# A second product added into its copy in place ahead of the last turns, and GpSimd in program order in the output projection

## The chip, the cores and the metric

The kernel runs on one core of a Trainium2 chip. The metric is the device time of one execution in microseconds (us). Three executions of the kernel before were timed, and one more was profiled.

## The reference

A decoder of two layers on 1,024 positions of width 1,024, in float32. Each layer mixes (sparse attention in the first layer, forgetting attention in the second, and a small cross-attention in both), projects the heads back onto the residual stream, normalizes it, and adds a gated feed-forward part with a causal convolution of width 3. What the change touches is the output projection and the start of the feed-forward part:

```python
x = x + jnp.concatenate([o_mix, o_mem], axis=-1) @ w_o[l]
x = x + conv_ffn(rms_norm(x, ffn_norm[l]), w_up[l], conv_w[l], conv_b[l], w_down[l])
# in conv_ffn
u = h @ w_up
u = lax.conv_general_dilated(u, conv_w[:, None, :], window_strides=(1,), padding=[(CONV_WIDTH - 1, 0)], ...) + conv_b
a, b = u[..., :D_FF], u[..., D_FF:]
return (jax.nn.silu(a) * b) @ w_down
```

## The kernel before

**Matmuls.** Every float32 operand is split into a rounded high part and the rest (`split`, lines 76 to 84: ScalarE writes the high part at L81, VectorE the low part at L82), and a product is three matmuls, L157, L158 and L159. So each operand costs one ScalarE and one VectorE instruction before TensorE can use it.

**Output projection** (`out_proj`). The residual stream `x` lies in SBUF as eight row tiles t = 0 to 7, in two column halves n. For each n and t, 24 matmuls fill a PSUM tile `psb`, which VectorE adds onto `x` (L871). In the second half (n = 1) a row tile is then complete, and `norm_part` follows: a DMA stores it (`xm`, L909), ScalarE sums its squares (L118), VectorE scales the sum (L119, `ss`), GpSimd raises it to the power -1/2 (L121, `rs`), and VectorE multiplies the tile by it in place (L911), which waits for the store too. From t = 4 on VectorE forms differences with the tile four below (L931, L932, L929) and GpSimd one more (L930). TensorE transposes the results (`turn_split`, L903, called a turn here) into `psb`, from where they are split into the operands of the next stage (`hx` and `hT`). The pool of `psb` has four buffers.

**Up-projection** (class `Up`). The product of the hidden state and `w_up` is made of seven half-size products per channel tile instead of eight (Strassen's scheme in Winograd's form), for NF = 22 pairs n of channel tiles. Pair n loads two weight blocks, `ra` and `rb` (L1272, 512 KB each, into the ring `wr` of three buffers). GpSimd forms sums of their halves: `sums_21` (L1279, L1280) and `sums_34` (L1286, L1287), each into one tile `ws` of a ring of two. ScalarE and VectorE split these and the weights themselves (`split_a`, `split_21`, `split_34`, `split_b`). The products of a pair go to the two halves `p` and `c` of a PSUM tile `psa`, of which there are two:

- `first` fills `p` and copies it to an SBUF tile c1 (L1320; tag `c`, a ring of three buffers).
- `second` fills another tile q, which `take_second` adds to c1 into `u` (L1338).
- `third` adds onto `p`, and copies it (L1320, c2). Product 3 fills `c` and is copied too (c5). Products 4, 5 and 6 follow.

For the pairs 0 and 1 `first` and `second` run inside `out_proj`, and there q is the half `c` of their `psa`. `u` lies in the pool of the feed-forward part, which takes the memory of `x` once the last turn has read it, so `take_second` of both pairs stands at the start of `run`, behind all turns.

**What waits for what.** The framework places a wait where two instructions touch the same tile, and takes a PSUM tile `psa` as one thing: product 3 of pair 0, which writes the half `c`, waits for `take_second(0)`, and for the copy c2 of the half `p`.

**What sets the order.** In `out_proj` the framework's scheduler orders the instructions of each engine. In `run` a table of slots (`todo`) does, and `manual_schedule` keeps VectorE and ScalarE in program order there.

Of the kernel before, what the change touches and what calls it, by code (L numbers as in the profile page):

```python
# [8 lines left out]
F32 = mybir.dt.float32  # L9
# [3 lines left out]
ALU = mybir.AluOpType  # L13
# [4 lines left out]
P = 128  # L18
D = 1024
S = 1024  # L20
NT = S // P
KT = D // P
CH = 512
# [19 lines left out]
class Trunk:  # L43
# [398 lines left out]
    def attention(self, ap, l, od, units, work, spare, lead=4, lag=2, lead_work=2):  # L442
# [79 lines left out]
        for k in range(first, len(steps) + lag + 4):  # L522
            st = steps[k] if 0 <= k < len(steps) else None
            run(k, "max")
            if st:
                self.turn_p(ap, st)
            run(k, "exp")
            if st:
                self.lower_p(st)
            run(k, "norm")  # L530
            while items and items[0]["at"] <= k:
                begin(k, items.pop(0))
            if k < 0 and lead_work and items:
                for _ in range(lead_work):
                    if work:
                        advance()
            if st and k < n_fill:
                owed += max(total, 0) / (n_fill - k)
                while owed >= 1 and work:
                    owed -= 1  # L540
                    advance()
            if 0 <= k - lag < len(steps):
                self.value(steps[k - lag])
                if steps[k - lag]["end"]:
                    finish(k, steps[k - lag]["u"])
            if not work and whole and k % 4 == 0:
                operand()
            if k == units[-1]["start"]:
                w_o = self.load_block(self.a["w_o"][l], [(0, CH)])
# [298 lines left out]
    def out_proj(self, l, oT, pool, fx, up):  # L848

        nc, a = self.nc, self.a
        (oT, w), B, late, gb = oT, up.B, [], None
        for n in range(2):
            if n:
                w = self.load_block(a["w_o"][l], [(CH, CH)])
                gb = self.wraw([P, D])
                nc.sync.dma_start(gb, a["ffn_norm"][l:l + 1, :].to_broadcast([P, D]))
                up.load(0)
            for t in range(NT):  # L860
                ps = self.psb()
                oh, ol = oT[t // 4]
                o = (t % 4) * P
                for kt in (0, 1, 2, 3, 4, 6, 7, 5):
                    self.mm3(ps, (oh[:, kt, o:o + P], ol[:, kt, o:o + P]), w(kt, 0, CH), kt == 0, kt == 5)
                if n == 0 and t == NT - 1:
                    up.conv_turn()
                if n and t == NT - 1:
                    up.split_a(0)
                xs = self.x[:, t, n * CH:(n + 1) * CH]  # L870
                nc.vector.tensor_tensor(xs, ps, xs, ALU.add)  # L871
                turns, late = late, self.norm_part(pool, fx, l, t, gb, B) if n else []
                if n and t in (2, 4):
                    (up.sums_21 if t == 2 else up.sums_34)(0)
                if n and t == 1:
                    turns, late = [], turns + late
                for f in turns:
                    f()
        up.load(1)
        up.first(0)  # L880
        up.second(0, True)
        late[0]()
        up.split_a(1)
        up.split_21(0)
        up.first(1)
        for f in late[1:]:
            f()
        up.second(1, True)
        for i in range(4):
            self.turn_split(self.x[:, 4 + i, CH:], B["t3"], i)  # L890
            self.turn_split(self.x[:, i, CH:], B["t4"], i)
            if i == 1:
                up.third(0)
                up.split_34(0)
                up.split_b(0)
                up.sums_21(1)
                up.sums_34(1)
# [226 lines left out]
    def gated(self, l, oT, src, fx):  # L1124

        tc = self.tc
        with tc.tile_pool(name=f"e{l}", bufs=1) as ep:
            up = Up(self, l, ep)
            with tc.tile_pool(name=f"x{l}", bufs=1) as xp:
                self.residual(xp, src)  # L1130
                self.out_proj(l, oT, xp, fx, up)
            down = Down(self, l, up.gds, fx)
            with tc.tile_pool(name=f"u{l}", bufs=1) as late, tc.manual_schedule(engines={mybir.EngineType.DVE, mybir.EngineType.Activation}):
                up.run(late, down)
        return down
# [64 lines left out]
    def run(self):  # L1200
        a, tc = self.a, self.tc
        self.constants()
        self.xd = self.dp.tile([S, D], F32, name="xd")
        self.xm = [self.dp.tile([S, D], F32, name=f"xm{l}") for l in range(2)]
        oT = self.layer1_attn(*self.middle(self.layer0()))
        with tc.tile_pool(name="fx1", bufs=1) as fx:
            down = self.gated(1, oT, self.xd, fx)
            with tc.tile_pool(name="y1", bufs=1) as yp:
                gb = []

                def each(j):
                    if j == 0:
                        gb.append(self.gain(yp, a["final_norm"].rearrange("(o n) -> o n", o=1)))
                    if j % 3 == 2:
                        self.final(yp, gb[0], j // 3)
                halves = {}

                def late(j):
                    if j == 0:
                        self.final(yp, gb[0], 3)  # L1220
                    if 2 <= j < 6:
                        halves[j + 2] = self.final_right(yp, gb[0], j + 2)
                self.down_all(1, down, yp, each, lambda: None, True, late)
                for t in range(4, NT):
                    self.final_left(yp, gb[0], t, *halves[t])


class Up:
# [106 lines left out]
    def take_second(self, n):  # L1335
        s, k = self.st[n], self.k
        s["ua"] = k.sb(self.late, [P, S], F32, "u", 3)
        k.nc.vector.tensor_tensor(s["ua"][:, :CH], s["q"], s["c1"], ALU.add)  # L1338

    def third(self, n):  # L1340
        s = self.st[n]
        self.prod(n, s["p"], "s2", "t2", False)
        s["c2"] = self.copied(s["p"])
# [64 lines left out]
    def run(self, late, down):  # L1408


        self.late = late
        done = {0: 3, 1: 3}
        self.split_21(1)
        self.take_second(0)
        self.take_second(1)
        self.third(1)
        todo = {}

        def at(slot, f, *args):
            todo.setdefault(slot, []).append(lambda: f(*args))  # L1420
        for slot, f in ((148, down.claim_x), (150, down.claim_x), (152, down.claim_h), (154, down.claim_h), (156, down.claim_h),
                        (158, down.claim_x), (160, down.claim_h)):
            at(slot, f)
        at(151, down.fetch, 3)
        for slot, n in ((151, 1), (153, 2), (155, 3), (159, 4)):
            at(slot, down.prep, n)
        for n in range(NF):
            for slot, f in ((-9, self.load), (-6, self.sums_21), (-3, self.sums_34), (-3, self.split_a), (-2, self.split_21),
                            (-1, self.split_b), (3, self.split_34)):
                if n > 1 or n == 1 and f in (self.split_b, self.split_34):  # L1430
                    at(7 * n + slot, f, n)
            for slot, h, tap in ((11, 0, 1), (12, 0, 0), (13, 1, 1), (14, 1, 0)):
                at(7 * n + slot, self.conv, n, h, tap)
            at(7 * n + 16, self.gate, n)
            if n % 2:
                at(7 * n + 17, self.left, n // 2)
                at(7 * n + 19, self.store, n // 2)
        for slot in range(7 * NF + 13):
            for f in todo.pop(slot, ()):
                f()  # L1440
            for n in (slot // 7 - 1, slot // 7):
                i, odd = divmod(slot - 7 * n, 2)
                if 0 <= n < NF and not odd and done.get(n, 0) <= i < 7:
                    self.product(n, i)
            if slot >= 7 * NF + 6:
                down.step()
        assert not todo
# [163 lines left out]
```

## Time and profile before

| what | value |
|---|---|
| median of the timed runs | 2577.46 us |
| the three runs | 2571.35, 2577.46, 2578.0 us |
| the profiled execution | 2576.98 us |
| its span in the trace | 2574.9 us |
| granted TensorE clock, mean | 0.99 |
| busy: TensorE, VectorE, ScalarE, GpSimd | 2467.4, 1880.5, 1347.7, 745.7 us |

The span starts with the first instruction in the trace and ends with the last; 2.1 us of the execution's time lie outside it. Busy time of TensorE counts matmuls that overlap each other. PE is TensorE, DVE VectorE, ACT ScalarE, POOL GpSimd, SP the engine that issues the DMAs. In a row of the timeline stand the start, the duration, the engine, the line, the instruction with what it writes and reads, and in brackets how long the engine sat idle before it and what ended that. Names are given without buffer numbers.

### The profile page before, as it was taken

The numbers are of one execution on the slowest core, as the hardware profiler recorded it, in microseconds if no ns is written. First come the engines' busy times: TensorE is split into PE (matmuls) and PEld (weight loads), VectorE is DVE, ScalarE is ACT, GpSimd is POOL, SyncE is SP. The second block draws the span as 40 slices with busy tenths as digits, with TensorE's granted clock in tenths as the row PEclk, the third lists the DMA queues.
The fourth block names the chain that finished last, engine by engine and source line by source line (L and its number), as shares of the span: only waits on it lengthen the run. The fifth ranks groups of instructions, "written<-read, shape, count | busy, mean of one in ns | idle before, by whom it ended". The sixth has DMA issues, their size and how long they took to land.

```text
span 2574.9 us, 35712 instructions
## 1 busy us (share of the span) xinstructions
PE 2467.4 (96%) x12306; PEld 2059.2 (80%) x12306; DVE 1880.5 (73%) x3180; ACT 1347.7 (52%) x2565; POOL 745.7 (29%) x616
## 2 busy tenths in 40 slices
PE   7898999988999999999999999999899999999998
PEld 6787877777778888887888988887677888888887
DVE  5757888887367878877766467878466787888866
ACT  5337777877145445444454356767234544545444
POOL 0104444544124554543000000000223555452000
PEclk9998999999999999999999999999999999999999
DMA  8473234433422323347334566766532332338523
GB/s 245 141 218 111 66 87 115 112 103 119 165 74 87 113 95 103 111 136 287 129 126 131 156 181 189 203 182 178 202 115 69 105 112 97 101 113 289 179 90 123
DMA packets 303276, 357.68 MB, mean 139 GB/s; under 512 B 38024, under 2 KB 183288, under 8 KB 303096
## 3 DMA queue, kind: packets, MB, share of 16 engines
q1 hardware_dynamic: 303096, 355.41, 43.8%
q8 instruction: 97, 1.59, 0.3%
q14 instruction: 83, 0.68, 0.1%
HBM read 245.55 MB, written 109.78 MB: 138 GB/s over the span
## 4 chain that ended last, share of the span: by engine, by line
PE 74%; DVE 8%; ACT 6%; DMA 5%; issue 3%; POOL 3%; SPq 1%; POOLq 0%; ACTq 0%; DVEq 0%
PE psa L157 12%; PE psa L158 12%; PE psa L159 12%; PE psb L157 9%; PE psb L159 9%; PE psb L158 9%; PE psa L300 4%; PE psb L399 4%; PE psb L422 4%; ACT pt L406 2%; DVE pt L409 2%; ACT ps L343 1%; DVE wl L82 1%; DVE ps L330 1%; POOL ws L1396 1%
## 5 line engine op out<-in xcount | busy, mean ns | idle before, releaser
L81 ACT ACTIVATE wh<-wr 128x512 fp32r<-128x512 f32 (+2 forms) x254 | 193.4, 765 | 330.1 <-PE psb L159 142.5
L82 DVE TENSOR_TENSOR wl<-wr,wh 128x512 fp32r<-128x512 f32 (+2 forms) x254 | 243.5, 963 | 141.3 <-ACT wh L81 140.5
L1377 DVE SCALAR_TENSOR_TENSOR v<-u,cw,v 128x1023 f32<-128x1023 f32 (+1 forms) x176 | 277.3, 1575 | 68.9 <-ACT v L1375 67.3
L409 DVE TENSOR_TENSOR pt<-psb,pt 128x512 fp32r<-128x512 f32 (+2 forms) x380 | 247.3, 660 | 70.1 <-ACT pt L406 66.9
L1375 ACT ACTIVATE v<-u,cw 128x1024 f32<-128x1024 f32 x88 | 109.8, 1248 | 310.2 <-DVE u L1364 283.5
L406 ACT ACTIVATE pt<-psb 128x512 fp32r<-128x512 f32 (+2 forms) x380 | 214.1, 574 | 92.2 <-PE psb L399 86.4
L422 PE MATMUL psb<-pt,vv 128*128 128x512 f32 (+2 forms) x864 | 227.3, 359 | 18.1 <-DVE pt L409 12.3
L157 PE MATMUL psa<-hT,wh 128*128 128x512 f32 x560 | 219.7, 393 | 5.3 <-DVE u L1338 5.3
L159 PE MATMUL psa<-hT,wl 128*128 128x512 f32 x560 | 219.0, 391 | 0.8 <-DVE wl L82 0.8
L158 PE MATMUL psa<-hT,wh 128*128 128x512 f32 x560 | 218.9, 391 | 0.0
L300 PE MATMUL psa<-kk,qq 128*128 128x512 f32 (+4 forms) x792 | 187.0, 351 | 15.5 <-DVE stat L330 7.7
L422 PEld LDWEIGHTS psb<-pt,vv 128*128 128x128 f32 x864 | 142.8, 193 | 43.0 <-DVE pt L409 20.5
L343 ACT ACTIVATE ps<-ps,stat 128x128 f32<-128x128 f32 (+1 forms) x192 | 148.1, 773 | 46.5 <-DVE stat L330 46.3
L481 POOL TENSOR_TENSOR wr<-wr 128x512 f32<-128x512 f32 x32 | 41.7, 1306 | 432.3 <-DMA kd<-st 246.1
L157 PE MATMUL psb<-hT,wh 128*128 128x512 f32 x384 | 156.8, 408 | 1.8 <-DVE pt L409 1.4
L1279 POOL TENSOR_TENSOR ws<-wr 128x512 f32<-128x512 f32 x44 | 72.2, 1640 | 295.6 <-DMA wr<-in_w_up_dram 243.3
L399 PE MATMUL psb<-consts,ps 128*128 128x128 f32 x928 | 149.0, 278 | 8.1 <-DVE pt L409 3.4
L121 POOL TENSOR_TENSOR rs<-ss,consts 128x1 f32<-128x1 f32 x40 | 23.0, 577 | 458.0 <-DVE ss L119 320.2
L159 PE MATMUL psb<-hT,wl 128*128 128x512 f32 x384 | 151.7, 395 | 0.0
L158 PE MATMUL psb<-hT,wh 128*128 128x512 f32 x384 | 151.0, 393 | 0.0
L330 DVE CUSTOM_DVE_ANT_0 ps<-psa,caub 128x128 f32<-128x128 f32 (+1 forms) x192 | 139.0, 751 | 15.0 <-PE psa L300 14.7
L300 PEld LDWEIGHTS psa<-kk,qq 128*128 128x128 f32 x792 | 123.0, 195 | 31.2 <-DVE stat L330 10.0
(299 smaller groups left out, 6822.5 us busy)
## 6 DMA issues: line engine op xcount, KB each, us to landing
wr<-in_w_up_dram SPq DMA_DIRECT2D x88, 512.0 KB
wr<-gd SPq DMA_DIRECT2D x154, 256.0 KB
gd<-v SPq DMA_DIRECT2D x88, 256.0 KB
o<-ob SPq DMA_DIRECT2D x128, 128.0 KB
wr<-o SPq DMA_DIRECT2D x32, 512.0 KB
hT<-in_w_down_dram SPq DMA_DIRECT2D x64, 256.0 KB
gd<-gs SPq DMA_DIRECT2D x60, 256.0 KB
qd<-st SPq DMA_DIRECT2D x56, 256.0 KB
```

What stands on the lines that cost most here:

```text
L81: nc.scalar.activation(hi, src, AF.Copy)
L82: nc.vector.tensor_tensor(lo, src, f32(hi), ALU.subtract)
L157: mm(out, lh, rh, start=first, stop=False, skip_group_check=more)
L158: mm(out, lh, rl, start=False, stop=False, skip_group_check=more)
L159: mm(out, ll, rh, start=False, stop=last, skip_group_check=more)
L300: nc.tensor.matmul(out, w, rhs, start=b not in banks[:i], stop=b not in banks[i + 1:])
L343: nc.scalar.activation(p, p, AF.Exp, bias=st[:, 0, ii:ii + 1], scale=-1.0, accum_out=st[:, 1, ii:ii + 1])
L399: nc.tensor.transpose(tp[0:kb, x:x + P], br["pt"][ii][:, o:o + kb], self.ident)
L406: nc.scalar.activation(st["hi"], st["src"], AF.Copy)
L409: self.nc.vector.tensor_tensor(st["lo"], st["src"], f32(st["hi"]), ALU.subtract)
L422: self.nc.tensor.matmul(out, v, t, start=st["begin"] and i == 0, stop=st["end"] and i == len(mms) - 1)
L1377: nc.vector.scalar_tensor_tensor(v[:, d:], u[:, :S - d], cw[:, tap, i:i + 1], v[:, d:], ALU.mult, ALU.add)
```

## The change

The addition of q to c1 is taken out of `run` and put into `out_proj`, as an addition in place (`take_early`): VectorE reads q and c1 and writes c1. What remains in `run` is a copy of the result into `u`, on GpSimd (`place_early`). And all of `out_proj` keeps GpSimd in program order.

```diff
         for f in late[1:]:
             f()
+        up.take_early(0)
         up.second(1, True)
+        up.take_early(1)
         for i in range(4):
...
-                self.out_proj(l, oT, xp, fx, up)
+                with tc.manual_schedule(engines={mybir.EngineType.Pool}):
+                    self.out_proj(l, oT, xp, fx, up)
...
+    def take_early(self, n):
+        s = self.st[n]
+        self.k.nc.vector.tensor_tensor(s["c1"], s["q"], s["c1"], ALU.add)
+
+    def place_early(self, n):
+        s, k = self.st[n], self.k
+        s["ua"] = k.sb(self.late, [P, S], F32, "u", 3)
+        k.nc.gpsimd.tensor_copy(s["ua"][:, :CH], s["c1"])
...
-        self.take_second(0)
-        self.take_second(1)
+        self.place_early(0)
+        self.place_early(1)
         self.third(1)
```

Both layers run this code. The lines of the changed kernel are some higher: L930 of before is L932, L911 is L913, L1279 to L1287 are L1282 to L1290, L1320 is L1323.

GpSimd, from the second half of the output projection of the first layer on, before. `rs` is the scale of a row tile, `ws` a weight sum of pair 0, `x<-x,t` the difference of L930:

```order
L1279 TENSOR_TENSOR ws_7636<-wr_7529 128x512
L1286 TENSOR_TENSOR ws_7756<-wr_7527,wr_7529 128x512
L121 TENSOR_TENSOR rs_7562<-ss_7559,consts 128x1
L1280 TENSOR_TENSOR ws_7636<-ws_7636,wr_7527 128x512
L1287 TENSOR_TENSOR ws_7756<-wr_7527,ws_7636 128x512
L121 TENSOR_TENSOR rs_7599<-ss_7596,consts 128x1
L121 TENSOR_TENSOR rs_7633<-ss_7630,consts 128x1
L121 TENSOR_TENSOR rs_7698<-ss_7695,consts 128x1
L121 TENSOR_TENSOR rs_7746<-ss_7743,consts 128x1
L930 TENSOR_TENSOR x_7278<-x_7278,t_1317_7753 128x512
L121 TENSOR_TENSOR rs_7804<-ss_7801,consts 128x1
```

The same place after:

```order
L121 TENSOR_TENSOR rs_7564<-ss_7561,consts 128x1
L121 TENSOR_TENSOR rs_7601<-ss_7598,consts 128x1
L121 TENSOR_TENSOR rs_7635<-ss_7632,consts 128x1
L1282 TENSOR_TENSOR ws_7638<-wr_7531 128x512
L1283 TENSOR_TENSOR ws_7638<-ws_7638,wr_7529 128x512
L121 TENSOR_TENSOR rs_7700<-ss_7697,consts 128x1
L121 TENSOR_TENSOR rs_7748<-ss_7745,consts 128x1
L1289 TENSOR_TENSOR ws_7758<-wr_7529,wr_7531 128x512
L1290 TENSOR_TENSOR ws_7758<-wr_7529,ws_7638 128x512
L121 TENSOR_TENSOR rs_7806<-ss_7803,consts 128x1
L932 TENSOR_TENSOR x_7278<-x_7278,t_1317_7755 128x512
```

The scales of the row tiles 0 to 2 stand ahead of pair 0's `sums_21` now, and its `sums_34` behind the scale of row tile 4. With it moves the load of pair 1's `ra`, which takes the buffer that `sums_34` reads: the DMA queue has it behind the stores of row tiles 0 to 4 now, and had it behind that of row tile 0.

GpSimd further on, at the end of the output projection, before. The sums with `wr_79..` are those of pair 1, with `wr_81..` those of pair 2:

```order
L930 TENSOR_TENSOR x_7278<-x_7278,t_1333_7867 128x512
L121 TENSOR_TENSOR rs_7928<-ss_7925,consts 128x1
L1279 TENSOR_TENSOR ws_8096<-wr_7959 128x512
L1280 TENSOR_TENSOR ws_8096<-ws_8096,wr_7957 128x512
L1286 TENSOR_TENSOR ws_8099<-wr_7957,wr_7959 128x512
L1287 TENSOR_TENSOR ws_8099<-wr_7957,ws_8096 128x512
L930 TENSOR_TENSOR x_7278<-x_7278,t_1343_7931 128x512
L1279 TENSOR_TENSOR ws_8180<-wr_8160 128x512
L1280 TENSOR_TENSOR ws_8180<-ws_8180,wr_8158 128x512
```

And after:

```order
L121 TENSOR_TENSOR rs_7930<-ss_7927,consts 128x1
L932 TENSOR_TENSOR x_7278<-x_7278,t_1333_7869 128x512
L932 TENSOR_TENSOR x_7278<-x_7278,t_1343_7933 128x512
L1282 TENSOR_TENSOR ws_8100<-wr_7961 128x512
L1283 TENSOR_TENSOR ws_8100<-ws_8100,wr_7959 128x512
L1289 TENSOR_TENSOR ws_8103<-wr_7959,wr_7961 128x512
L1290 TENSOR_TENSOR ws_8103<-wr_7959,ws_8100 128x512
L1282 TENSOR_TENSOR ws_8185<-wr_8165 128x512
L1283 TENSOR_TENSOR ws_8185<-ws_8185,wr_8163 128x512
L1350 COPY u_8145<-c_7976 128x512
L1350 COPY u_8147<-c_8018 128x512
```

The sums of pair 1 stand behind the difference of row tile 7 now, and the two copies into `u` behind pair 2's `sums_21`, which waits for the load of pair 2's `rb`.

VectorE at row tile 7, before, with `wl<-ws` the low parts of pair 0's `split_34` and then of pair 1's `split_21`:

```order
L911 SCALAR_TENSOR_TENSOR x_7278<-x_7278,rs_7928,wr_7525 128x1024
L82 TENSOR_TENSOR hT_7750<-psb_7950,hT_7750 128x4x128
L931 TENSOR_TENSOR x_7278<-x_7278 128x512
L82 TENSOR_TENSOR wl_8089<-ws_7756,wh_8088 128x1024
L932 TENSOR_TENSOR t_1343_7931<-x_7278 128x512
L82 TENSOR_TENSOR hx_7567<-psb_7988,hx_7567 128x4x128
L929 TENSOR_TENSOR x_7278<-t_1343_7931,x_7278 128x512
L82 TENSOR_TENSOR wl_8137<-ws_8096,wh_8136 128x1024
```

And after:

```order
L913 SCALAR_TENSOR_TENSOR x_7278<-x_7278,rs_7930,wr_7527 128x1024
L82 TENSOR_TENSOR hT_7752<-psb_7952,hT_7752 128x4x128
L933 TENSOR_TENSOR x_7278<-x_7278 128x512
L1345 TENSOR_TENSOR c_7976<-psa_7963,c_7976 128x512
L934 TENSOR_TENSOR t_1343_7933<-x_7278 128x512
L82 TENSOR_TENSOR hx_7569<-psb_7990,hx_7569 128x4x128
L931 TENSOR_TENSOR x_7278<-t_1343_7933,x_7278 128x512
L82 TENSOR_TENSOR wl_8093<-ws_7758,wh_8092 128x1024
L82 TENSOR_TENSOR hT_7751<-psb_8022,hT_7751 128x4x128
L82 TENSOR_TENSOR hT_7752<-psb_8029,hT_7752 128x4x128
L82 TENSOR_TENSOR wl_8142<-ws_8100,wh_8141 128x1024
L1345 TENSOR_TENSOR c_8018<-psa_8005,c_8018 128x512
```

The first addition in place (L1345) stands where the low part of pair 0's `split_34` stood, which comes behind the differences of row tile 7 now. Pair 1's `split_21` stands two splits of a turn later, on ScalarE too, and the second addition follows it. Before, both additions stood behind the last eight splits of turns. On TensorE, `third(1)` runs whole ahead of product 3 of pair 0 now; before, three matmuls of that product stood ahead of it. The second layer shows the same moves.

## The prediction

> **What bounds the kernel now.** The page first:
>
> ```profile
> PE 2467.4 (96%) x12306; PEld 2059.2 (80%) x12306; DVE 1880.5 (73%) x3180; ACT 1347.7 (52%) x2565; POOL 745.7 (29%) x616
> PE 74%; DVE 8%; ACT 6%; DMA 5%; issue 3%; POOL 3%; SPq 1%; POOLq 0%; ACTq 0%; DVEq 0%
> ```
>
> TensorE is busy for 96% of the span and carries 74% of the chain that ended last. An edit on the other engines counts where TensorE stands idle for them, and by how long. So next the timeline of TensorE around the change, the rows in which it stood idle ahead of a turn or of product 3. The last four are the second layer.
>
> ```profile
> 702.11 1.26 PE L903 MATMUL psb<-consts,x 128*128 128x128 f32 x8 [2.22 <-DVE x L911]
> 745.33 0.65 PE L903 MATMUL psb<-consts,x 128*128 128x128 f32 x4 [0.22 <-DVE x L911]
> 748.85 0.63 PE L903 MATMUL psb<-consts,t 128*128 128x128 f32 x4 [1.04 <-DVE t L932]
> 761.78 0.77 PE L157 MATMUL psa<-hT,wh 128*128 128x512 f32 x1 [2.64 <-DVE u L1338]
> 1887.48 1.26 PE L903 MATMUL psb<-consts,x 128*128 128x128 f32 x8 [0.89 <-DVE x L911]
> 1929.78 0.66 PE L903 MATMUL psb<-consts,x 128*128 128x128 f32 x4 [0.22 <-DVE x L911]
> 1933.30 0.63 PE L903 MATMUL psb<-consts,t 128*128 128x128 f32 x4 [1.01 <-DVE t L932]
> 1946.25 0.77 PE L157 MATMUL psa<-hT,wh 128*128 128x512 f32 x1 [2.64 <-DVE u L1338]
> ```
>
> Three groups: the turns of row tile 1 (702, 1887), those of row tile 7 (745 and 749, 1930 and 1933), and product 3 of pair 0, which waits for `take_second` (762, 1946).
>
> A long wait costs more than itself. Here are matmuls behind the first wait and undisturbed ones; the windows behind three waits (the granted clock is the third figure from the end); and two copies of ScalarE, c2 of pair 0, which starts when `third(0)` ends, and c5, which starts when product 3 of pair 0 ends:
>
> ```profile
> 703.31 0.73 PE L157 MATMUL psb<-wh,hT 128*128 128x512 f32 x1
> 707.07 0.40 PE L157 MATMUL psb<-wh,hT 128*128 128x512 f32 x1
> 709.16 0.39 PE L157 MATMUL psb<-wh,hT 128*128 128x512 f32 x1
> 709.84 0.39 PE L157 MATMUL psb<-wh,hT 128*128 128x512 f32 x1
> 704.00:706.00 2.00, 2.00 (x7) 1.52 (x6) 1.67 (x4) 1.36 (x3) 0.55 (x1) 0.50 0.40 164
> 762.00:764.00 2.00, 2.00 (x5) 1.58 (x6) 0.23 (x1) 0.00 (x0) 0.00 (x0) 0.50 0.00 0
> 1946.20:1948.00 1.80, 1.75 (x4) 1.49 (x5) 0.50 (x1) 0.00 (x0) 0.00 (x0) 0.50 0.00 0
> 1888.00:1890.00 2.00, 2.00 (x12) 1.52 (x11) 0.99 (x4) 1.88 (x4) 0.46 (x1) 1.00 0.56 227
> 757.43 0.60 ACT L1320 ACTIVATE c<-psa 128x512 f32<-128x512 f32 x1 [2.15 <-PE psa L159]
> 768.99 0.60 ACT L1320 ACTIVATE c<-psa 128x512 f32<-128x512 f32 x1 [0.93 <-PE psa L159]
> ```
>
> From 709.16 to 709.84 three matmuls start, so one takes 0.227 us at full clock. From 703.31 to 707.07 there are nine; at full clock they take 2.04 us, here 3.76: 1.7 us lost at a clock of 0.50. From 761.78 to 768.99 lie the 24 matmuls of `third(1)` and product 3, at full clock 5.45 us, here 7.21: 1.75 us lost, and the same is taken for 1946, where the clock is 0.50 too. After the wait of 0.89 us it is 1.00: nothing lost there. Between `third(0)` and the wait, from 757.43 to 759.14, lie the last four turns: 1.7 us, or 0.43 a turn.
>
> **The change part by part.** *The head (A).* The scale of row tile 0 no longer stands behind two weight sums on GpSimd.
>
> ```profile
> 691.52 1.31 POOL L1279 TENSOR_TENSOR ws<-wr 128x512 f32<-128x512 f32 x1 [43.66 <-DMA wr<-in_w_up_dram]
> 694.51 0.56 POOL L121 TENSOR_TENSOR rs<-ss,consts 128x1 f32<-128x1 f32 x1
> 690.63 0.15 DVE L119 TENSOR_SCALAR ss<-ss 128x1 f32<-128x1 f32 x1 [1.54 <-ACT junk L118]
> 691.97 1.42 DVE L82 TENSOR_TENSOR vl<-wr,vh 128x512 fp32r<-128x512 f32 x1 [1.18 <-ACT vh L81]
> 695.11 2.30 DVE L911 SCALAR_TENSOR_TENSOR x<-x,rs,wr 128x1024 f32<-128x1024 f32 x1 [1.72 <-POOL rs L121]
> 700.77 1.28 DVE L911 SCALAR_TENSOR_TENSOR x<-x,rs,wr 128x1024 f32<-128x1024 f32 x1 [1.33 <-DMA xm<-x]
> ```
>
> `ss` is ready at 690.78, `rs` was done at 695.07; now it is by 691.5. VectorE then scales row tile 0 once the low part `vl` is through, at 693.4, in 1.28 us instead of 2.30: done at 694.7, not 697.41, 2.7 us earlier. The chain of row tile 1 starts behind it, and its store, which ended its wait, starts with it. So its scaling ends 2.7 us earlier too, and the wait of 2.22 us goes whole, with 1.7 us of low clock. In the second layer 0.89 goes. A = 2.2 + 1.7 + 0.9 = 4.8 us. If something else held row tile 1, nothing goes: 0 to 4.8.
>
> Pair 0's sums, moved past the scales, are used by splits that stand on ScalarE behind this row, and so is the load of pair 1's `ra`, moved past four stores:
>
> ```profile
> 733.16 2.22 ACT L81 ACTIVATE wh<-wr 128x1024 fp32r<-128x1024 f32 x2
> ```
>
> The load starts near 721 now, after `sums_34`, and takes 4 us (below): 8 us to spare, so nothing.
>
> *Row tile 4 (D).* `sums_34` of pair 0 stands behind the scale of row tile 4 now, and runs while VectorE makes that tile's differences:
>
> ```profile
> 720.50 1.28 DVE L911 SCALAR_TENSOR_TENSOR x<-x,rs,wr 128x1024 f32<-128x1024 f32 x1
> 722.55 0.69 DVE L932 TENSOR_TENSOR t<-x 128x512 f32<-128x512 f32 x1
> 723.42 0.69 DVE L871 TENSOR_TENSOR x<-psb,x 128x512 f32<-128x512 f32 x1 [0.18 <-PE psb L159]
> ```
>
> A collision is shown twice: L911 takes 2.30 us beside GpSimd's sums (above) and 1.28 without, and L931 1.17 (below) against 0.69. So 1.0 + 0.5 = 1.5 us later on VectorE. TensorE ends its matmuls at 723.4 and does one turn (0.43) before it needs L932, done at 723.24: 0.6 us to spare. D costs 0.9 at most by these rows and 0 if they miss each other; I take 0.8 a layer, since they start within a microsecond: -1.6. The Trainium skill (SBUF — State Buffer, Who interferes with whom) speaks against the change here: a VectorE instruction with two SBUF inputs and a GpSimd instruction that reads SBUF hold the shared port pair one after the other, the loser waiting for the whole of the other. By that rule two sums of 1.3 us could cost 2.0 us a layer and the kernel would take about 2567; the trace agrees that both slow down.
>
> *Row tile 7 (B).* The sums of pair 1 no longer run beside these:
>
> ```profile
> 743.26 2.01 DVE L911 SCALAR_TENSOR_TENSOR x<-x,rs,wr 128x1024 f32<-128x1024 f32 x1
> 745.80 1.17 DVE L931 TENSOR_TENSOR x<-x 128x512 f32<-128x512 f32 x1
> 746.89 1.21 DVE L82 TENSOR_TENSOR wl<-ws,wh 128x1024 fp32r<-128x1024 f32 x1
> 748.03 0.68 DVE L932 TENSOR_TENSOR t<-x 128x512 f32<-128x512 f32 x1
> ```
>
> L911 loses 0.73, L931 0.48, and the addition (0.69) in the place of `wl` 0.52: L932 ends at 747.0, not 748.71. That is 1.7 us, more than the waits of 0.22 + 1.04, and of 0.22 + 1.01: B = 2.5. Its bounds are 0 and 2.5.
>
> *Product 3 (C).* The last two additions ran on VectorE behind eight splits; now TensorE finds `c` free. C = 2 x (2.64 + 1.75) = 8.8 us, before what is late next.
>
> *The last turns (E).* ScalarE's split of pair 1's `sums_21` waits for GpSimd, as it did, but stands ahead of the last turns' splits now:
>
> ```profile
> 746.45 1.07 ACT L81 ACTIVATE wh<-ws 128x1024 fp32r<-128x1024 f32 x1 [4.43 <-POOL ws L1280]
> 752.60 3.67 DVE L82 TENSOR_TENSOR hT<-psb,hT 128x512 fp32r<-128x512 f32 x6
> 751.55 2.27 POOL L930 TENSOR_TENSOR x<-x,t 128x512 f32<-128x512 f32 x1
> 749.83 1.76 POOL L1287 TENSOR_TENSOR ws<-wr,ws 128x512 f32<-128x512 f32 x1
> 755.55 1.31 POOL L1279 TENSOR_TENSOR ws<-wr 128x512 f32<-128x512 f32 x1 [1.73 <-DMA wr<-in_w_up_dram]
> L366 POOL TENSOR_SCALAR ps<-ps,stat,gates 128x512 f32<-128x512 f32 x12 | 9.3, 774 | 0.0
> ```
>
> In the times of before, leaving the earlier gain out: from 747.0 GpSimd does L930 and two sums, 1.31 each when alone, 2.27 at worst; at 752 they are done, the split at 753.1, then VectorE's `wl` (1.2), the second addition (0.7) and four low parts of 0.6, to 757.5. The last four turns wait for those buffers of `psb`. TensorE would reach the end of the turns at 759.14 - 1.26 = 757.9. I take 0.8 us a layer, 0 to 1.9 by GpSimd's two prices: E = -1.6.
>
> *The copies (F).* The ring of c1 has three buffers, so c2 of pair 1 waits for the first copy on GpSimd and c5 of pair 0 for the second, and TensorE for both ahead of product 4. The copies stand behind pair 2's `sums_21`, which waits for the load of `rb`, which waits for pair 1's `sums_34`. From 752 two more sums end at 755.3 with some collision; the load takes from 751.59 to 755.55, 4.0 us: 759.3; two sums: 761.9; two copies, which the trace doesn't show on GpSimd, 0.77 each by the one-input row of the same size, and at worst 2.27: 763.5. TensorE ends product 3 at 757.9 + 0.8 + 5.45 = 764.1, c5 is copied by 764.7, and four matmuls of the other pair's product 3 cover it. I take 0.3 a layer: F = -0.6.
>
> Sum: 4.8 + 2.5 + 8.8 - 1.6 - 1.6 - 0.6 = 12.3 us. The profiled execution took 2576.98, 0.5 below the median: 2564.7. TensorE bounds the rest, so the gain is kept to the end.
>
> **The rivals.** About 0.3%, 7.7 us, is what a measurement of this kernel can tell from no change: faster means below 2569.7.
>
> *The copies take the place of the wait (0.14).* If product 4 starts no earlier than before (768.99 + 0.60 = 769.6, against 765.0), B, C and E are gone: 4.8 - 1.6 = 3.2 us, 2573.8. For it: a chain of five GpSimd steps and one load with under a microsecond to spare. Against: it needs 4.6 us more than the bare prices.
>
> *Slower by the same chain (0.07).* Everything collides: five steps of 2.27 from 747.0 end at 758.3, the load at 762.3, sums and copies at 771.4, c5 at 772.0: 2.4 us a layer later than before. With row tile 4 at 2.0, 4.8 - 4.0 - 4.8 = -4.0: 2581. It decides from 771.2 on, where 1.6 us a layer eat what A and D leave.
>
> *The clock stays low (0.08).* The clock fell behind 8 + 8 transposes with the wait between, 1.26 + 2.22 + 1.26 = 4.7 us without another matmul, and behind four turns and a wait, 1.7 + 2.64 = 4.3, but not behind 1.26 + 0.89 + 1.26 = 3.4. The last turns with E are 1.7 + 0.8 = 2.5 us, at worst 3.6. If the limit is near that, 2 x 1.75 of C and 2 x 1.1 more of E go: 6.6 us, 2570.4. The Trainium skill (TensorE: Matmul & The Clock Gate, Part 1) has TensorE throttled after an idle window of about 3.4 us; the trace agrees if transposes count as idle.
>
> *The order isn't what held row tile 1 (0.06).* A is 0: 7.5 us, 2569.5, on the border.
>
> **How the numbers follow.** My forecast, 2564.7, has 0.60, and a range of its own from 2560.9 (D, E and F at 0) to 2569. The range to 2574 takes in the first, third and fourth rival. Faster: 0.60 + 0.03 = 0.63. Within 0.3%: 0.03 + 0.14 + 0.08 + 0.07 = 0.32. Slower: 0.05, for what no row here prices.
>
> **What would show it.** Right: no wait of TensorE for L911 at row tile 1, none for the first addition, full clock behind the last turns, L911 of row tile 7 at 1.28 us. D: a wait for L932 (now L934) at row tile 4. Wrong: TensorE idle behind product 3 for ScalarE's c2 or c5, with GpSimd's copies ahead of them, or a granted clock of 0.50 there.

## The result, and the profile after

The changed kernel took 2559.93 us (median of 4 runs, 2559.14 to 2565.91) against 2575.68 for the kernel before in the runs beside it: ratio 0.9944, 95% interval 0.9931 to 0.9956, or 11 to 18 us faster. Run again later it took 2558.43 (6 runs), ratio 0.9941 (0.9922 to 0.9959). The forecast was 2564.7 in a range of 2560 to 2574, and 12.3 us of gain; the median lies at the low edge of the range, and below the 2560.9 that the prediction gave for D, E and F at nothing. Whether the six terms of the sum are right is not seen in the total, so the traces come first.

The page of the changed kernel, the lines that answer to those of before:

```profile
PE 2460.7 (96%) x12306; PEld 2052.7 (80%) x12306; DVE 1868.4 (73%) x3180; ACT 1345.1 (53%) x2565; POOL 764.1 (30%) x620
PE 73%; DVE 8%; ACT 6%; DMA 5%; issue 3%; POOL 3%; SPq 1%; POOLq 0%; ACTq 0%; DVEq 0%
```

It tells nearly nothing: TensorE is the bound as before. The timeline of TensorE does tell. These are all rows in the two stretches that show a wait of over 0.3 us, then the sixteen transposes of the last turns, the last matmul of product 3 of pair 0 and the first of product 3 of pair 1:

```profile
712.47 0.63 PE L905 MATMUL psb<-consts,t 128*128 128x128 f32 x4 [1.10 <-DVE t L934]
1882.00 1.09 PE L905 MATMUL psb<-consts,x 128*128 128x128 f32 x8 [0.57 <-DVE x L913]
1890.10 0.63 PE L905 MATMUL psb<-consts,t 128*128 128x128 f32 x4 [1.07 <-DVE t L934]
...
744.82 2.51 PE L905 MATMUL psb<-consts,x 128*128 128x128 f32 x16
752.42 0.39 PE L159 MATMUL psa<-hT,wl 128*128 128x512 f32 x1
752.69 0.50 PE L157 MATMUL psa<-hT,wh 128*128 128x512 f32 x1
```

The eight waits that the prediction showed are gone: none at row tile 1, none at row tile 7, none for the first addition (psa is entered at 747.08, behind the last turns, without a wait). A wait for L934 at row tile 4 is new in each layer, 1.10 and 1.07 us, as term D said. The 0.57 is row tile 3's in the second layer, which stood at 0.46 before. The granted clock (third figure from the end) was 1.00 where it had been 0.50:

```profile
700.00:702.00 2.00, 2.00 (x11) 1.64 (x10) 1.12 (x4) 0.83 (x3) 0.55 (x1) 1.00 0.56 225
747.00:750.00 3.00, 3.00 (x16) 2.49 (x15) 1.95 (x4) 0.90 (x2) 1.25 (x1) 1.00 0.30 90
```

Where D comes from, on GpSimd and on VectorE at row tile 4:

```profile
707.48 1.32 POOL L1289 TENSOR_TENSOR ws<-wr,wr 128x512 f32<-128x512 f32 x1
708.76 2.29 POOL L1290 TENSOR_TENSOR ws<-wr,ws 128x512 f32<-128x512 f32 x1
708.04 1.84 DVE L913 SCALAR_TENSOR_TENSOR x<-x,rs,wr 128x1024 f32<-128x1024 f32 x1
709.91 1.69 DVE L933 TENSOR_TENSOR x<-x 128x512 f32<-128x512 f32 x1
711.63 0.69 DVE L934 TENSOR_TENSOR t<-x 128x512 f32<-128x512 f32 x1
```

The scaling takes 1.84 (1.28 before), the first difference 1.69 (0.69 before) and the second sum 2.29 (1.31 alone): both sides lose. And at the end of the stretch, ScalarE's split of pair 1, VectorE's low part of it with the eight low parts behind, GpSimd's copies, and ScalarE's c2 of pair 1:

```profile
741.24 1.06 ACT L81 ACTIVATE wh<-ws 128x1024 fp32r<-128x1024 f32 x1 [3.21 <-POOL ws L1283]
742.33 1.23 DVE L82 TENSOR_TENSOR wl<-ws,wh 128x1024 fp32r<-128x1024 f32 x1 [1.08 <-ACT wh L81]
744.08 4.86 DVE L82 TENSOR_TENSOR hT<-psb,hT 128x512 fp32r<-128x512 f32 x8
751.39 1.18 POOL L1350 COPY u<-c 128x512 f32<-128x512 f32 x2
752.04 0.60 ACT L1323 ACTIVATE c<-psa 128x512 f32<-128x512 f32 x1 [4.08 <-POOL u L1350]
```

The low parts of the turns stand behind a low part that waits for GpSimd; that is E. ScalarE's c2 waits 4.08 us for the copy and ends at 752.64; TensorE starts product 3 of pair 1 at 752.69. That is F, and nothing is to spare: the same 0.05 us lies between c2 and TensorE in the kernel with three copies (below), where TensorE does wait for c2. Here it starts 0.27 us behind the matmul ahead of it, and not 0.227 (0.38 in the second layer).

To price the terms, the two stretches were cut at six matmuls that are the same in every trace (their starts before: 691.59, 709.16, 735.25, 751.60, 758.87, 771.82, and 1878.29, 1892.91, 1919.71, 1936.06, 1943.34, 1956.30). The times between them, first layer / second layer, in us, with the price forecast:

| piece | before | after | gain | forecast |
|---|---|---|---|---|
| row tile 1 (A) | 17.57 / 14.63 | 13.49 / 13.52 | 5.2 | 4.8 |
| row tiles 3 to 5 (D) | 26.09 / 26.80 | 27.68 / 28.45 | -3.2 | -1.6 |
| row tile 7 (B) | 16.35 / 16.34 | 14.67 / 14.65 | 3.4 | 2.5 |
| `third(0)` and last turns (E) | 7.27 / 7.28 | 8.00 / 8.00 | -1.5 | -1.6 |
| `third(1)`, product 3 (C, F) | 12.95 / 12.96 | 8.81 / 8.90 | 8.2 | 8.8 and -0.6 |

Together 12.1 us, where the forecast had 12.3. The spans differ by 16.5 (2574.9 and 2558.4), so 4.4 us of this pair of profiles lie elsewhere. 1.4 of it is a wait for the weights at the head of the second layer (below). For the rest the clock has to be understood.

### The profile page after: what moved, and what is told of

Its sections match the earlier page's. It is cut to its first block, busy times and chain, and to the rows that moved or that the text cites. A ratio compares the mean times of both kernels' runs of the same rounds, so it can differ in the third digit from the quotient of the medians.

```text
span 2558.4 us, 35716 instructions
## 1 busy us (share of the span) xinstructions
PE 2460.7 (96%) x12306; PEld 2052.7 (80%) x12306; DVE 1868.4 (73%) x3180; ACT 1345.1 (53%) x2565; POOL 764.1 (30%) x620
## 4 chain that ended last, share of the span: by engine, by line
PE 73%; DVE 8%; ACT 6%; DMA 5%; issue 3%; POOL 3%; SPq 1%; POOLq 0%; ACTq 0%; DVEq 0%
PE psa L157 11%; PE psa L158 11%; PE psa L159 11%; PE psb L157 9%; PE psb L159 9%; PE psb L158 9%; PE psb L399 4%; PE psa L300 4%; PE psb L422 4%; DVE pt L409 2%; POOL ws L1408 2%; ACT pt L406 1%; DMA hT<-in_w_down_dram 1%; DVE ps L330 1%; DVE wl L82 1%
## 5 line engine op out<-in xcount | busy, mean ns | idle before, releaser
L1389 DVE SCALAR_TENSOR_TENSOR v<-u,cw,v 128x1023 f32<-128x1023 f32 (+1 forms) x176 | 271.7, 1544 | 69.0 <-ACT v L1387 68.8
L157 PE MATMUL psa<-hx,wh 128*128 128x512 f32 x368 | 144.0, 392 | 0.4 <-ACT u L1379 0.4
```

The lines of the kernel that those rows point to most:

```text
L157: mm(out, lh, rh, start=first, stop=False, skip_group_check=more)
L1389: nc.vector.scalar_tensor_tensor(v[:, d:], u[:, :S - d], cw[:, tap, i:i + 1], v[:, d:], ALU.mult, ALU.add)
```

## The experiments

**Each half alone.** The first kernel has GpSimd's program order and no early addition:

```
-                self.out_proj(l, oT, xp, fx, up)
+                with tc.manual_schedule(engines={mybir.EngineType.Pool}):
+                    self.out_proj(l, oT, xp, fx, up)
```

> Program order on GpSimd alone, on the kernel before; the two additions stay where they were. Theory 1 (the terms are local and add up): the wait ahead of row tile 1 goes in both layers (A, 5.3 us as the two traces show it), a wait of about 1.1 us for the second difference of row tile 4 comes in each layer (D, 3.1 us with what follows it), part of row tile 7 is won (B, about 2), and the waits of 2.64 us for the first addition stay in both layers (C not won): about 4 us faster than before, 2571.5. Theory 2 (the order on GpSimd is not what held row tile 1, the additions did all): a wait of about 2 us ahead of row tile 1 stays in the first layer, and only D is left: 2575 to 2579.

It took 2569.15 us (12 runs), ratio 0.9975 (0.9963 to 0.9987). Its rows of TensorE:

```profile
716.11 0.63 PE L903 MATMUL psb<-consts,t 128*128 128x128 f32 x4 [1.10 <-DVE t L932]
752.86 0.47 PE L157 MATMUL psa<-hT,wh 128*128 128x512 f32 x1 [2.63 <-DVE u L1339]
```

No wait at row tile 1, the wait of D in its place, and the 2.63 us for the first addition still there. By pieces, against the first profile of before: A 5.2, D -2.5, B 3.0. So theory 1 holds, and nearly all of B is the order's.

The second has the additions and copies without the order (the `with` line taken out of the changed kernel):

> The two additions in place ahead of the last turns and the two copies on GpSimd, but GpSimd's order left to the scheduler as before. Theory 1 (local terms): the waits of 2.64 us for the first addition go in both layers (C, 8.2 us), the wait ahead of row tile 1 stays (2.2 and 0.9 us), there is no wait for the second difference of row tile 4, and row tile 7 keeps its collision with pair 1's sums: 8 to 10 us faster than before, 2566 to 2568. Together with the kernel that has the order alone the gains make 12 to 14. Theory 2 (the two halves need each other: without the order, pair 1's sums or the copies come too late): product 3 or 4 waits for GpSimd instead, and it gains under 4 us: above 2571.5.

It took 2566.43 us (6 runs), ratio 0.9959 (0.9945 to 0.9973). The piece of C gains 8.55, that of B 1.05, and the wait ahead of row tile 1 stays:

```profile
692.45 1.97 PE L905 MATMUL psb<-consts,x 128*128 128x128 f32 x8 [2.39 <-DVE x L913]
738.19 0.63 PE L905 MATMUL psb<-consts,t 128*128 128x128 f32 x4 [0.51 <-DVE t L934]
```

Theory 1 again. E shows in neither half (the piece of the last turns takes 7.06 us in both, 8.00 with both): it is a price of having them together.

**D: the sums one row tile earlier.**

```
-                if n and t in (2, 4):
+                if n and t in (2, 3):
```

> The changed kernel with pair 0's second pair of weight sums one row tile earlier (behind the scale of row tile 3 and not of row tile 4). Theory 1 (D is the collision of these sums with row tile 4's scaling and first difference): those two take 1.28 and 0.69 us again, the wait of 1.1 us for the second difference goes in both layers, and the kernel is 2 to 3 us faster than the changed one: about 2557.5. Theory 2 (a collision only moves): row tile 3's scaling takes 2.2 us instead of 1.28 in the first layer and TensorE waits for it about as long: no gain, 2560 or above. Theory 3 (row tile 4 waits for something else): the wait for the second difference stays.

It took 2560.61 us (6 runs, 2552.72 to 2564.23), ratio 0.9932 (0.9917 to 0.9948): the runs can't tell it from the changed kernel (0.9941, 0.9922 to 0.9959 in the set behind). The trace can. VectorE at row tile 4, and TensorE's wait there:

```profile
713.89 1.28 DVE L913 SCALAR_TENSOR_TENSOR x<-x,rs,wr 128x1024 f32<-128x1024 f32 x1
715.21 0.69 DVE L933 TENSOR_TENSOR x<-x 128x512 f32<-128x512 f32 x1
...
724.19 0.63 PE L905 MATMUL psb<-consts,t 128*128 128x128 f32 x4 [0.16 <-DVE t L934]
```

Both are back at 1.28 and 0.69; the 1.10 is gone, and the 0.16 is row tile 5's, which stays. The piece is 26.43 / 26.95 and the one of row tile 1 unchanged at 13.49: the cause of the wait at row tile 4 is shown. The collision moves on to row tile 3, whose scaling takes 1.79 us now, but TensorE doesn't wait for that.

**The clock.** The prediction took a low clock to follow when TensorE had no matmul but transposes for over 3.4 us. To test this, the kernel before was given each transpose of the last four turns twice:

```
-        for k in range(4):
+        for k in [0, 1, 2, 3] * times:
             self.nc.tensor.transpose(
```

> The kernel before, with each transpose of the last four turns made twice into the same place, so that TensorE is busy for 1.7 us of the 2.64 that it waits for the first addition. Theory K1 (the clock of one fixed period of 3.41 us is set by TensorE's busy share of the period before, transposes counted: the traces show 0.50 behind shares of 0.10 to 0.45 and 1.00 behind 0.61 and more in most periods): the wait shrinks to about 0.9 us, the share stays above 0.6, the clock stays 1.00 there in both layers, and the kernel is 3.4 us faster than before: about 2572.3. Theory K2 (the forecast's: over 3.4 us without a matmul other than a transpose drops the clock): the stretch without one is 4.3 us as before, the clock falls to 0.50 there in both layers, no gain: 2575.7.

It took 2570.26 us (12 runs), ratio 0.9983 (0.9973 to 0.9992), 2 to 7 us faster for more work. (VectorE also makes the first addition one low part earlier here, which is part of why the wait below is shorter.) The wait for the first addition, and then the two clock periods around it in each layer:

```profile
751.21 0.47 PE L157 MATMUL psa<-hT,wh 128*128 128x512 f32 x1 [1.23 <-DVE u L1338]
```

```profile
747.13:750.54 3.41, 2.85 (x27) 2.61 (x24) 2.15 (x4) 2.32 (x4) 0.10 (x1) 1.00 0.00 0
750.54:753.96 3.42, 2.75 (x12) 2.31 (x13) 1.72 (x3) 0.07 (x1) 0.00 (x0) 1.00 0.02 5
1928.14:1931.55 3.41, 3.20 (x30) 2.96 (x28) 1.79 (x3) 2.31 (x5) 0.37 (x1) 1.00 0.00 0
1931.55:1934.97 3.42, 2.40 (x11) 2.00 (x12) 2.07 (x4) 0.43 (x1) 0.00 (x0) 1.00 0.02 5
```

TensorE is busy for 70 to 94% of them and the clock stays at 1.00, though no matmul other than a transpose ran for as long as before. The forecast's rule for the clock (K2) is wrong; K1 holds. What K1 says can be read in before's own trace, whose clock changes only at times a whole number of 3.413 us apart. Periods of before, then of a later profile of the same kernel (the second figure is TensorE's busy time):

```profile
700.00:703.41 3.41, 1.30 (x9) 0.94 (x9) 2.48 (x3) 0.74 (x2) 0.07 (x1) 1.00 0.05 18
703.41:706.83 3.42, 3.42 (x8) 2.65 (x9) 2.56 (x5) 1.95 (x5) 0.55 (x1) 0.50 0.37 153
...
758.02:761.44 3.42, 1.12 (x11) 0.88 (x9) 2.89 (x5) 1.97 (x5) 0.21 (x1) 1.00 0.00 0
761.44:764.85 3.41, 3.07 (x7) 2.51 (x8) 0.79 (x2) 0.00 (x0) 0.00 (x0) 0.50 0.00 0
```

```profile
748.57:751.99 3.42, 2.07 (x18) 1.74 (x16) 1.94 (x4) 2.56 (x5) 1.13 (x1) 1.00 0.00 0
751.99:755.40 3.41, 2.12 (x9) 1.80 (x10) 1.74 (x3) 0.00 (x0) 0.00 (x0) 1.00 0.00 0
755.40:758.81 3.41, 3.41 (x17) 2.82 (x16) 0.65 (x1) 1.12 (x2) 0.00 (x0) 1.00 0.00 0
```

In the first profile the wait for the first addition lies inside one period, TensorE is busy for 1.12 of 3.42 us, and the next period runs at 0.50. In the later one the same wait of 2.64 us falls across the edge at 751.99, both periods are busy for 61%, and the clock stays. Where the edges fall differs from run to run.

**The changed kernel again**, for its spread and its clock:

> The changed kernel once more, as it is, beside the other kernels of this set. Theory 1 (the change is worth 12 to 13 us in its own stretches, and the rest of the 16.5 us between the first two profiles came from clock periods of 0.50 elsewhere, 11 before and 9 after): the median is 2560 to 2563, TensorE's waits in the two stretches are those of the first profile (0 at row tile 1 of the first layer, 1.1 at row tile 4, none at product 3), and the periods of 0.50 elsewhere come in another number and at partly other places. Theory 2 (all 16 us are the change's): the same places elsewhere are at 0.50, and the median is 2559 to 2560.

It took 2558.43 us. The pieces are those of the first profile within 0.3 us, but for D in the second layer (27.68 for 28.45); the periods of 0.50 elsewhere stand at partly other places (566, 624 and 1430 us new, 219 gone). Theory 1, though the median came out below its range.

**F: each copy three times.**

```
+        for _ in range(3):
             k.nc.gpsimd.tensor_copy(s["ua"][:, :CH], s["c1"])
```

> The changed kernel with each of the two copies made three times, in turn (copy 1, copy 2, and again twice). Theory 1 (the copies cost nothing but stand just in time: ScalarE's c2 of pair 1 ended 0.05 us before TensorE began product 3 of pair 1): copy 1 is last done four copies of 0.59 us later, 2.4 us, and TensorE waits 2.3 us ahead of product 3 of pair 1 in each layer, with a period of 0.50 behind it in some: 4.6 to 8 us slower than the changed kernel, 2565 to 2568. Theory 2 (the copies have the slack of several microseconds): no wait of TensorE there, the time is the changed kernel's.

It took 2566.88 us (12 runs), ratio 0.9972 (0.9959 to 0.9985): 8.4 us above the changed kernel beside it. In the pieces 4.4 us of that show, all in `third(1)` and product 3; no period of 0.50 stands behind the wait, and the rest of the 8.4 isn't placed. TensorE ahead of product 3 of pair 1, ScalarE's c2, and the copies:

```profile
759.12 0.50 PE L157 MATMUL psa<-hT,wh 128*128 128x512 f32 x1 [2.02 <-ACT c L1323]
758.47 0.60 ACT L1323 ACTIVATE c<-psa 128x512 f32<-128x512 f32 x1 [6.22 <-POOL u L1351]
755.60 3.40 POOL L1351 COPY u<-c 128x512 f32<-128x512 f32 x6
```

Four more copies ahead of c2 are 2.27 us at 0.57 each, and 2.02 of them come out as a wait (1.87 in the second layer). Theory 1: the first rival of the prediction had the right mechanism, and a slack of 0.2 us at most kept it from coming. Where TensorE meets it is product 3 of pair 1, though, and not product 4, as the prediction had it.

**E: the low parts first.** Program order on VectorE at the last turns, with the split of pair 1 behind the first four turns (it goes out of `run` for that, and pair 0's `split_34` and `split_b` move ahead of the block):

```
+        with self.tc.manual_schedule(engines={mybir.EngineType.DVE, mybir.EngineType.Pool}):
+            for i in range(4):
+                self.turn_split(self.x[:, 4 + i, CH:], B["t3"], i)
+                self.turn_split(self.x[:, i, CH:], B["t4"], i)
+                if i == 1:
+                    up.third(0)
+                    up.sums_21(1)
+                    up.sums_34(1)
+                    up.split_21(1)
```

> The changed kernel with VectorE's order at the last turns changed: the low parts of the four turns ahead of them stand before the low part of pair 1's split, not behind it. Theory 1 (E: the last turns wait for their buffers because that low part waits for GpSimd's sums): the 16 transposes of the last turns take 1.8 to 1.9 us and not 2.51, in both layers, and the kernel is about 1.3 us faster than the changed one. Theory 2 (the wait moves to the third product of pair 1, which needs that low part): TensorE waits 0.6 us or more ahead of its third matmul, no gain.

```profile
748.73 1.91 PE L907 MATMUL psb<-consts,x 128*128 128x128 f32 x16
746.91 2.48 DVE L82 TENSOR_TENSOR hT<-psb,hT 128x512 fp32r<-128x512 f32 x4 [0.97 <-ACT hT L81]
749.31 1.22 DVE L82 TENSOR_TENSOR wl<-ws,wh 128x1024 fp32r<-128x1024 f32 x1
```

The last turns take 1.91 us, their piece 7.24 / 7.25 for 8.00, and no wait comes behind: theory 1 for the cause. The time, 2559.41 us (6 runs; 0.9945, 0.9929 to 0.9962), can't show 1.5 us.

**Both edits**, the sums and the low parts:

> Both edits together: the sums of pair 0 one row tile earlier and the low parts first. Theory 1 (D and E are apart, so their prices add): no wait of 1.1 us at row tile 4, the last turns in 1.9 us, and 4 us faster than the changed kernel run beside it: about 2556 to 2558. Theory 2 (TensorE only comes sooner to the next wait, for pair 1's split or for c2 behind GpSimd's copies): a new wait of 1 us or more ahead of the third product or of product 3 of pair 1, and the time of the kernel with the sums alone.

It took 2556.03 us (6 runs, 2553.02 to 2559.0), ratio 0.9931 (0.9914 to 0.9948): the fastest here, 2.4 us under the changed kernel's median in the same set, with overlapping intervals. The five pieces add up to 4.7 us less than in the changed kernel's first profile, 3.7 less than in its second. The prices add.

**Filling a wait elsewhere.** If a low clock costs 1.7 us a period, filling other long waits of TensorE should pay. Ten matmuls of zeros were put where it waits some 3 us for the first gated tiles, in the kernel before and in the kernel with both edits; they add zero to an accumulator:

```
+        if (i, j) == (1, 4):
+            zero = k.m_cau
+            for _ in range(10):
+                k.nc.tensor.matmul(self.banks[i][0], zero[:, :P], zero[:, :CH], start=False, stop=False, skip_group_check=True)
```

> The kernel before, with ten matmuls of zeros (128x512) added to an accumulator of the down projection ahead of the place, far from the change, where TensorE waits about 3 us for the first gated tiles read back in each layer (1212 and near 2394 us of the first profile; in eight traces one or two periods of 0.50 stand behind that wait, 15 of 16 times). The result isn't changed. Theory K1 (a fixed period's clock is set by the busy share of the period before): the ten matmuls fill some 2.3 us of the wait, the wait left is about 1 us, the clock there is 1.00 in both layers, and the kernel is 3.4 to 5 us faster than before: 2571 to 2573. Theory K3 (the clock falls for a reason other than the busy share there, as reading back from memory or the long wait of ScalarE): 0.50 stays behind it, and the time is that of before, 2576, or above by what the ten matmuls delay.

> The changed kernel with both edits (pair 0's sums one row tile earlier, the low parts first) and the ten matmuls of zeros. Theory K1: 3.4 to 5 us faster than the kernel with both edits (2556.0): 2551 to 2553, no 0.50 behind the wait for the gated tiles. Theory K3: 2556.

The first is slower for it: 2579.02 us (12 runs), ratio 1.0016 (1.0007 to 1.0025). The second took 2560.54 us (5 runs), ratio 0.9947 (0.9934 to 0.9960), which is 4.5 us above the kernel with both edits in another set, with overlapping intervals. The clock did what K1 says: in the twelve traces without the fill a period of 0.50 stands there in 23 of 24 places, in the two with it in none of 4. (The 24th is the second layer of before's first profile. It has no wait at that place at all: some 170 matmuls around it take 39.4 us, and 44.8 in each of the other two profiles of before.) But the second kernel's rows there read, first TensorE, then VectorE:

```profile
1194.22 2.10 PE L1553 MATMUL psa<-caub 128*128 128x512 bf16 x9
1197.27 0.49 PE L157 MATMUL psa<-wh 128*128 128x512 f32 x1 [0.95 <-ACT wh L81]
1198.08 0.50 PE L158 MATMUL psa<-wl,wh 128*128 128x512 f32 x1 [0.31 <-DVE wl L82]
1211.32 0.50 PE L158 MATMUL psa<-wl,wh 128*128 128x512 f32 x1 [1.45 <-DVE wl L82]
1206.37 3.69 DVE L1534 TENSOR_TENSOR hT<-hT,hx 128x512 f32<-128x512 f32 x6
1209.98 0.68 DVE L82 TENSOR_TENSOR wl<-wr,wh 128x512 fp32r<-128x512 f32 x1
```

VectorE at the same place with both edits alone:

```profile
1204.09 1.89 DVE L1534 TENSOR_TENSOR hT<-hT,hx 128x512 f32<-128x512 f32 x3
1205.89 0.68 DVE L82 TENSOR_TENSOR wl<-wr,wh 128x512 fp32r<-128x512 f32 x1
```

The wait of 0.31 us stands in six traces without the fill too. The one of 1.45 us is new, and comes in both layers of both kernels (1.45 to 1.49). With the ten matmuls VectorE does its instructions in another order at this place, and only there: six sums (L1534) in a row, 3.69 us, ahead of the low part `wl` that TensorE needs, where it did three. So the experiment changed two things, the wait and VectorE's order. From a little ahead of this place to some 160 matmuls further, the two layers take 89.5 us in this kernel; with both edits alone they take 89.6, with two low periods in each layer, and with the low parts first 87.0, with one in each. The two new waits, 2.9 us together, are more than the 2.5 by which this kernel is behind the last. What filling the wait is worth with VectorE's order kept isn't shown, nor how much of the 4 us by which the runs are slower comes from the order.

**Was before's first profile typical?** In the second layer row tile 1's wait is 0.89 us in it, but 1.8 to 2.1 in three variants with the same order on GpSimd (early additions alone, doubled transposes, zeros). Twice more the kernel before:

> The kernel before, unchanged, profiled once more. Theory 1 (its first profile was not typical at row tile 1 of the second layer: TensorE had just waited 0.64 and 0.53 us for its weights, which took as much from the wait of 0.89 behind it): here the weights are in time, the wait ahead of row tile 1 is 2.1 us and a period of 0.50 stands behind it, so that the stretch from there to row tile 2 takes about 17 us and not 14.6. Theory 2 (0.89 us is typical of this kernel, and the 2.1 us belong to the variants): 0.89 and 14.6 again.

> The same once more, for the same question: theory 1 gives a wait of 2.1 us ahead of row tile 1 in the second layer in this profile too, theory 2 one of 0.89.

The first of the two:

```profile
753.28 0.47 PE L157 MATMUL psa<-hT,wh 128*128 128x512 f32 x1 [2.64 <-DVE u L1338]
1862.39 0.73 PE L157 MATMUL psb<-wh,hT 128*128 128x512 f32 x2 [0.46 <-ACT wh L81]
1863.65 0.50 PE L158 MATMUL psb<-wl,hT 128*128 128x512 f32 x1 [0.53 <-DVE wl L82]
1877.93 1.26 PE L903 MATMUL psb<-consts,x 128*128 128x128 f32 x8 [0.65 <-DVE x L911]
```

The waits were 0.65 and 0.64: theory 1 fell, the forecast's 0.89 was no accident. The weights come late, and shorten the wait behind them, in all three profiles of before and in the kernel with the order alone (26 matmuls from there take 7.45 to 7.86 us), and in time in every other trace (6.08 to 6.22), the changed kernel's among them. That is worth 1.4 us, which the forecast didn't have. What makes this load land sooner isn't settled, nor that it is the change: in the two kernels of before with doubled transposes and with zeros the load is in time as well, and there the wait ahead of row tile 1 is 2.07 and 2.13 us.

## Why the prediction was right, point by point

With three profiles of before and two of the changed kernel the terms come to (C and F share a piece; F is what it takes beyond the 17.4 us of the traces in which TensorE didn't wait for the copies):

| term | forecast | measured |
|---|---|---|
| A, row tile 1 | 4.8 | 4.7 |
| B, row tile 7 | 2.5 | 3.4 |
| C, product 3 | 8.8 | 7.8 |
| D, row tile 4 | -1.6 | -3.3 |
| E, last turns | -1.6 | -1.5 |
| F, copies | -0.6 | -0.2 |
| the weights of the second layer | none | 1.4 |
| sum | 12.3 | 12.3 |

The mean spans differ by 12.9 us (2573.1 and 2560.2), the means of all runs listed with a clock by 15.1 (56 of before in the experiments, 2575.2; 10 of the changed kernel, 2560.1). The executions of before scatter by 3.4 us (standard deviation), so the profiles were a few us lucky or unlucky; that the sum agrees to 0.1 us is luck as well, since three of its terms were off by 0.9 to 1.7 and these cancel with the 1.4 that the forecast didn't have. Between the sum and the 15.1 of the runs some 3 us are left that no term carries; part of it may be the clock (last section), and the rest stays open.

- **A** was right in place and price. The order alone shows it: no wait at row tile 1. The fourth rival (the order isn't what held it) is out.
- **B** was the sum of the waits, 1.26 a layer; the pieces gained 1.7. A wait on the timeline counts from the end of a matmul of 0.39 us, while the next would have started 0.227 behind its start; so by these two rows each wait costs about 0.16 us more than its figure, or 0.33 for two. One sign named for B did not come: row tile 7's scaling took 1.72 us and not 1.28, beside GpSimd's L932 of row tile 6, and the rest of the chain had enough to spare.
- **C** was right in its waits. Its clock price, 1.75 us each time, assumed that the clock falls behind each such wait. In the three profiles of before it did in 4 of 6 places; the piece takes 11.55 us without and 12.95 to 13.21 with it, so a low period costs 1.4 to 1.7 there.
- **D** is the step that was mis-sized. The delay on VectorE was put at 1.5 us with 0.6 to spare, so 0.9 at most and 0.8 taken. The delay came as priced: in the traces of the changed kernel L913 and L933 lose 0.56 and 1.0 in the first layer. But the wait is 1.10 and TensorE 1.27 us late by it, so some 0.3 were to spare and not 0.6; and row tile 5, which the sum left out, costs 0.3 more, so that the piece is 1.6 us longer. The page of the Trainium skill that spoke against the change (SBUF — State Buffer, Who interferes with whom: the loser of the shared port pair waits for the whole of the other instruction) had led to 2.0 a layer. The rows fit taking turns, but not that sum, which counted both of GpSimd's sums whole: L913 begins in the middle of the first and loses only 0.56, so VectorE's delay is 1.56 us and not 2.6. Putting the sums one row tile earlier shows the cause for row tile 4; row tile 5's 0.3 stays there, and its cause is open.
- **E** was right in mechanism and price, and the low parts first show it.
- **F** was priced 0.3 a layer. It cost 0.1 to 0.2 in the first profile of the changed kernel and nothing in the second (8.81 / 8.90 and 8.71 / 8.68 for the piece, 8.67 / 8.68 with the low parts first): a copy takes 0.57 to 0.63 us and not 0.77. With 0.2 us of slack at most, the rival that the copies take the wait's place was closer than its 0.14 says, and three times the copies brought it about.
- **The clock** stayed high, so the third rival didn't come. Its reason was wrong, and with it half of the explanation of C and A; the numbers survived because the waits behind which it was charged were long enough to empty a period most of the time.

## What to carry to other kernels

Price a change at fixed instructions that stand in both traces, not by the two spans: here terms of a few us repeat to some tenths, while executions of one kernel differ by 12. A wait of TensorE of 2 us or more is worth its length and, by chance, one slower period behind it, as long as nothing else is late behind it; and an edit on one engine can change the order on another, so compare the orders before reading the time. When work is moved between engines that slow each other down, count the delay on both sides and then look which copy or split now ends just in time: its slack is the next price.

## What the runs showed of the hardware

The granted clock is set for periods of 3.413 us whose edges don't move within a run, by how busy TensorE was in the period before, transposes counted. In 14 traces (periods at full clock, from 35 us to the last matmul), by that busy share:

| busy share | periods | next one at 0.50 |
|---|---|---|
| under 0.40 | 69 | 69 |
| 0.40 to 0.50 | 43 | 38 |
| 0.50 to 0.60 | 61 | 18 |
| 0.60 to 0.70 | 165 | 2 |
| 0.70 and above | 9829 | 0 |

The Trainium skill (TensorE: Matmul & The Clock Gate, Part 1) tells of a free-running window of 3413 ns and of an idle window as what throttles it: the traces agree with the window and its length, but a period half idle is enough. This is also most of the scatter between executions: the runs of before whose mean clock was 0.989 took 2578.8 us on average (7 runs), those at 0.993 2570.5 (6 runs). As an estimate from the mean clock of each run (one minus the clock, times the span), before loses 23.9 us to it on average and the changed kernel 18.7: three periods of 1.7 us fewer. Behind the waits removed stand 7 periods of 0.50 in the three profiles of before, 2.3 in each, so most of the three are theirs.
